# A decoder layer on one core: the convolution table padded from 1408 to 2048 bytes a partition

## The chip, the cores and the metric

One core of a Trainium2 chip runs the kernel in one launch. The metric is the device time of one execution in microseconds (us). In the text, PE is TensorE (matrix products), PEld its loading of stationary operands, DVE is VectorE, ACT ScalarE, POOL GpSimd, SP the queue that issues all the DMAs of this kernel. A matmul has a *stationary* operand (128x128, a slice of the weights) and a *moving* operand (here mostly 128x512 four-byte values, so 2048 bytes of each partition).

## The reference

One layer for 512 positions of width 2048, all in float32:

```python
proj = einsum(rmsnorm(x), w_in)                      # 2048 -> 5376, split into heads of A, B, C
out_a = banded_attention(...)                        # A: 8 heads, window 128, sinks
out_b = stick_breaking_attention(...)                # B: 8 heads
out_c = dilated_attention(...)                       # C: 16 heads, three dilations
mix = concat(rmsnorm(out_a), rmsnorm(out_b), rmsnorm(out_c))
x = x + einsum(mix, w_out)                           # 2048 -> 2048
u = causal_dwconv(einsum(rmsnorm(x), w_up), conv_w, conv_b)   # 2048 -> 2 * 5632, width 3 along the positions
gate, up = split(u, 2)
x = x + einsum(silu(gate) * up, w_down)              # 5632 -> 2048
```

The convolution needs 4 numbers a channel (3 taps and a bias) for 88 tiles of 128 channels: 352 columns of four bytes, 1408 bytes a partition. This is the table of the change.

## The kernel before

Activations lie with channels on the partitions and the 512 positions along the row, so one tile of 128 channels takes 2048 bytes a partition. Every large product is made of three matmuls per tile of 128 input channels, to keep float32 accuracy: the weights and the activations are each split into a high and a low part, and `mm3` (lines 263 to 267) issues high x high, high x low, low x high into one PSUM bank, 512 columns each. `product` (291) makes one output tile out of 16 input tiles (48 matmuls), or of 8 (24 matmuls), or in the last chunk of w_down of 4 (12 matmuls).

The weights come in pieces of 512 KB through the tile `wr` (3 buffers); ACT writes the high half `wh`, DVE the low half `wl` (`split`, 251). The order of all instructions is laid down when the program is built, by a list of tasks with estimated times; it depends on shapes and not on addresses.

The stages, in the order of time:

- The projection w_in with the heads of A, B and C beside it. Moving operands of the projection are the tiles `x` of the pool `xp`.
- The output projection of the heads of B and A (`project_ab`), moving operand again in `x` tiles.
- `fp`, the pool of the rest, is opened at line 908, in the room of the pool `ap` of the attention. Its first tile is the convolution table `conv`. `mix_split` (919) loads the heads of C into tiles `xg2` and splits them into tiles `mc`; the output projection of C then reads `mc` as moving operand, 16 products of 24 matmuls, and `projected` (933) writes the normalised result in `xg2`, high and low.
- The feed-forward: six chunks of up to 8 tiles of 128 channels. A tile of w_up, gate and up side, takes two products of 48 matmuls with moving operand `xg2` (88 products in all). `up` (988) puts silu(gate) * up, high and low, into tiles `x` in chunks 0, 2, 4 and into tiles `mc` in chunks 1, 3, 5 (line 992); the products of w_down (16 per chunk) read them as moving operand. The products of w_down of one chunk run between those of w_up of the next: two of w_up, then two of w_down, and so on.

Where the tiles lie, in bytes from the start of a partition, as the program places them, and the offset modulo 2048 at which they begin:

| tiles | pool | from | modulo 2048 |
|---|---|---|---|
| wr, wh, wl (3 x 4096, 4 x 2048, 4 x 2048) | wp | 10720 | 480 |
| x (32 x 2048) | xp | 39392 | 480 |
| st (9), sq, qs of the attention, 2048 each | ap | 106976 to 139744 | 480 |
| conv (1408) | fp | 104928 | 480 |
| xg2 (32 x 2048) | fp | 106336 | 1888 |
| rg, sq, acc, cv of the feed-forward, 2048 each | fp | 171872 to 225120 | 1888 |
| mc (16 x 2048) | fp | 178016 | 1888 |

A stationary operand is 512 bytes of a partition: slice k of a piece of `wh` or `wl` begins at 480 + 512 k. 480 + 1408 = 1888 is where the offset of the tiles behind `conv` comes from. The pool ends at 227168.

Of the kernel before, what the change touches and what calls it, by code (L numbers as in the profile page):

```python
# [9 lines left out]
F32 = mybir.dt.float32  # L10
# [10 lines left out]
EPS = 1e-6  # L21
NEG = -1e30

# columns of the packed small parameters
SM_AG, SM_FG, SM_MG, SM_G4, SM_SINK, SM_CONV, SM_N = 0, 16, 32, 48, 52, 60, 60 + 88 * 4
# columns of the packed constants
C_ID, C_ONE, C_MASK, C_TRI = 0, 128, 256, 384
NB = 640
# the least spacing of the heads of A, B, C, and what is added to each estimate
GAP = (8, 10, 10)  # L30
MARGIN = 0.08
# the order of the units of A and C
ORDER = "ACACACACCCCC"
# the order in which the output projection takes the tiles of heads: B, A, C
MIX_ORDER = list(range(4, 8)) + list(range(4)) + list(range(8, 16))


class Engine:
    """An engine whose instructions are timed by estimate as they are issued."""

    def __init__(self, clock, engine, cost):
        self.clock, self.engine, self.cost = clock, engine, cost
# [34 lines left out]


class Clock:
    """Issues tasks beside the stream of matrix products, in the order of the estimated times:  # L80
    a task yields when what it has issued has to end before it goes on (or a time to wait)."""

    def __init__(self):
        self.end = 0.0
# [32 lines left out]
def program(tc, xT, w_in, w_out, w_up, w_down, small, table, consts, onehot, lognum, out):  # L117
# [24 lines left out]
    with ExitStack() as ctx:  # L142
# [21 lines left out]
        gacc = [cp.tile([128, S], F32, name="gacc", bufs=2) for _ in range(2)]  # L164
        gacc.append(gacc[1])

        # a slot is taken before its tile is made and given back after the tile's last use
        total = {"pj": 2, "s": 4, "po": 1, "c": 1, "qs": 3, "st": 9, "akv": 4, "vt": 2, "av": 1, "strip": 2,
                 "sc": 3, "pt": 6, "sq": 6, "o": 2, "mx": 3, "dn": 3, "nm": 3, "es": 2,
                 "cv": 3, "acc": 1, "rg": 1}  # L170
        # the shapes of the slots that are not rows
        shapes = {"sc": [128, 1280], "pt": [128, 1664], "vt": [128, 4, 2, 2, 64], "av": [128, 4, 2, 2, 64],
                  "mx": [128, 4], "dn": [128, 4], "nm": [128, 4], "es": [128, 4]}
        free = {tag: list(range(n)) for tag, n in total.items()}
# [27 lines left out]
            slots = [held.pop(id(t)) for t in tiles]  # L202
            spawn(back(slots, max(clock.end - clock.now(), 0.01)))

# [1 line left out]
        b_units = [(10 + p, 6 + p, 14 + p) for p in range(4)]  # L206
        c_units = [(26 + p, 18 + p, 34 + p) for p in range(8)]
        tiles_in = [t for u in b_units[1:] for t in u] + [4, 5]
# [22 lines left out]
        at = {"load": 0, "split": 0, "use": 0}  # L231
# [8 lines left out]
                at["load"] = i + 1  # L240

        def split_next():
            """the next half of a piece of the weights"""
            i = at["split"]
            if i // 2 < len(stream):
                at["split"] = i + 1
                raw, arrival = raws[i // 2]
                n = raw.shape[1] // 2
                spawn(split(raw[:, i % 2 * n:i % 2 * n + n], arrival, i))
# [22 lines left out]
            return grab(ps, "pj")  # L272

        def accumulate(pt, acts, ks, each=None):
            """the k tiles ks of a tile of a product, with the next weights of the stream"""
            half = min(len(acts), 8) // 2
            for k in ks:
                while acts[k] not in ready:
                    idle()
                if k % half == 0:  # L280
                    while at["use"] not in parts:
                        idle()
                    hi, lo = parts.pop(at["use"])
                    at["use"] += 1
                    split_next()
                mm3(pt, hi, lo, k % half, ready[acts[k]], k == 0, k == len(acts) - 1)
                if each:
                    each(k)
                clock.run()

        def product(acts, after):
            """one tile of a product; then the task after(tile)"""
            pt = begin()
            accumulate(pt, acts, range(len(acts)))
            spawn(after(pt))
            clock.run()

# [1 line left out]
        def rstd(pool, ss, n):  # L299
            """-2n * (ss / n + EPS) ** -0.5, with a Newton step after the tables"""  # L300
            y, a = yield from take(pool, "sq", 2)
            scalar.activation(y, ss, AF.Ln, bias=epsc, scale=1.0 / n)
            scalar.activation(y, y, AF.Exp, scale=-0.5)
            yield
            gpsimd.tensor_mul(a, y, y)
            yield
            vector.scalar_tensor_tensor(a, ss, n * EPS, a, op0=ALU.add, op1=ALU.mult)
            give(ss)
            vector.scalar_tensor_tensor(a, a, -3.0 * n, y, op0=ALU.add, op1=ALU.mult)
            give(y)  # L310
            return a
# [28 lines left out]
        vector.memset(epsc, EPS)  # L340
        vector.memset(onec, 1.0)

# [1 line left out]
        with ExitStack() as actx:  # L344
            ap = actx.enter_context(tc.tile_pool(name="ap", bufs=1))

            def strips():
                """the biases of the heads that softmax takes, in their order, as far ahead as there is room"""
                for head in strip_order:
                    g = yield from take(ap, "strip")  # L350
                    a = rb[head:head + 1, 0:1]
                    load(g, bass.AP(tensor=a.tensor, offset=a.offset, ap=[[1, 128], [1, S]]))
                    yield
                    ready["strip", head] = g
# [6 lines left out]
            HALF = (slice(0, 64), slice(64, 128))  # L361

            def stacked(q, key):
                """for each head of the pair its high parts over its low parts"""
                res = yield from take(ap, "st", 2, F32R)
                for h in range(2):
                    scalar.copy(res[h][HALF[h]], q[HALF[h]])
                yield
                for h in range(2):
                    vector.tensor_sub(res[h][HALF[1 - h]], q[HALF[h]], res[h][HALF[h]].bitcast(F32))  # L370
                give(q)
                yield
                ready[key] = res

            def doubled(q, key):
                """for each head of the pair its high parts twice and its low parts twice"""
                tag = "akv" if key[0] == "ak" else "st"
                res = yield from take(ap, tag, 4, F32R)
                res = [res[:2], res[2:]]
                for h in range(2):  # L380
                    scalar.copy(res[h][0][HALF[h]], q[HALF[h]])
                yield
                for h in range(2):
                    vector.tensor_sub(res[h][1][HALF[h]], q[HALF[h]], res[h][0][HALF[h]].bitcast(F32))
                give(q)
                yield
                for x in range(2):
                    for h in range(2):
                        load(res[h][x][HALF[1 - h]].bitcast(F32), res[h][x][HALF[h]].bitcast(F32))
                    yield  # L390
                yield
                ready[key] = res
# [72 lines left out]
            def softmax_head(q, dup, vt, h, o, head, sinks, window):  # L465
# [52 lines left out]

                def place(t, i, n):
                    if window:  # L520
                        # block (j, i) at 256 j + 128 (i - j), the last one after its zeros
                        base, step = ((0, 128), (128, 128), (384, 128), (640, 256))[i]
                    else:
                        # block (j, i) at 384 j + 128 i
                        base, step = 128 * i, 384
                    b = t[:, base:base + 1]
                    return bass.AP(tensor=b.tensor, offset=b.offset, ap=[b.ap[0], [step, n // 128], [1, 128]])
# [29 lines left out]
                yield  # L557
                yield from head_out(po, h, o)

            # key blocks j of the stick-breaking heads: (j, first query, number of queries, column); in the operands of  # L560
            # products the last block follows columns of zeros
            BLK = [(0, 0, 512, 0), (1, 128, 384, 512), (2, 256, 256, 896), (3, 384, 128, 1152)]
            WIDE = [(0, 512, 0), (128, 384, 512), (256, 256, 896), (256, 256, 1408)]

# [78 lines left out]
                yield  # L643
                yield from head_out(po, h, o)

            # heads in the order in which they run, at most three at a time
            heads = []
            running = {"n": 0, "last": -100}
            outs = {}
# [40 lines left out]
                return stick_head(q[h], k[h], vt, h, o)  # L690

            def spill(g):
                """the normalised heads of a group in high and low parts, to wait for the slots of x"""
                tiles = (range(4), range(4, 8))[g]
                rg = yield from take(ap, "acc")
                yield from row_rstd(ap, gacc[g], 128 * len(tiles), rg)
# [26 lines left out]
                    strip_order.append(head)  # L723
            spawn(starter())

            # x and the first three tiles of w_in, tile of x by tile of x
            acc = grab(ap, "o")
            xg = [("x", k) for k in range(KT)]
            first = [grab(ps, "s"), grab(ps, "s"), grab(ps, "s")]
# [112 lines left out]
            spilled = []  # L842

            def last_products(q_after, v_after):
                """the last two tiles, by halves of x, so that half of its slots are free early"""
                q, v = begin(), begin()
                accumulate(q, xg, range(8))
                accumulate(v, xg, range(8), mix_load)
# [25 lines left out]
                else:  # L874
                    product(xg, normed(0, False, stacked, ("aq", p)))

            # the output projection of the heads of B and A, beside the last heads of C
            xn = []

            def project_ab(m):  # L880
# [20 lines left out]
            while left[2]:  # L901
# [2 lines left out]
                    m += 1  # L904
                else:
                    idle()
# [1 line left out]
        fp = ctx.enter_context(tc.tile_pool(name="fp", bufs=1, reuse_waits="tile"))  # L908
        cv = fp.tile([128, SM_N - SM_CONV], F32, name="conv")
        load(cv, small[:, SM_CONV:])  # L910

        rg = []

# [42 lines left out]
        for m in range(KT):  # L956
            product([("mix", i) for i in MIX_ORDER[8:]], projected(m))

# [1 line left out]
        gs = {}  # L960

        def conv(t, f, use):
# [80 lines left out]


def _pieces(w):
    """[K, N] as pieces of eight K tiles by one N tile, each [128, 8 * 128]"""
    k, n = w.shape
    w = w.reshape(k // 1024, 8, 128, n // 128, 128).transpose(3, 0, 2, 1, 4)
    return np.ascontiguousarray(w).reshape(n // 128 * (k // 1024), 128, 1024)
# [48 lines left out]
```

## Time and profile before

| | us |
|---|---|
| median of 3 runs (2267.1 to 2267.99) | 2267.95 |
| span of the profiled execution, first to last instruction | 2265.6 |
| PE busy in it | 2254.7 |
| DVE busy | 1211.2 |
| ACT busy | 981.9 |
| output projection of C (`mc` moving) | 700.38 to 789.97 |
| feed-forward | 789.97 to the end |

The busy time of PE counts a matmul from its start to its modelled end, and matmuls overlap, so that a stretch of back-to-back matmuls shows 100% whatever its pace. The pace is read from starts: the time from the start of one matmul to the start of a later one, divided by the number of matmuls begun between them.

### The profile page before, as it was taken

To read this page: it belongs to the slowest core of one execution; us is meant where nothing else is said; L and a number is where in the kernel's file an instruction comes from. 1 tells how busy PE (TensorE), PEld (TensorE's weight loads), DVE (VectorE), ACT (ScalarE), POOL (GpSimd) and SP (SyncE) were. 2 spreads that over 40 slices of the span, in tenths; PEclk is the share of its full clock that TensorE was granted. 3 is DMA by queue.
4 is the path that set the end of the run, shared out by engine and by line. 5 is a ranking of instruction groups with operands and counts; after the bars stand their busy time and mean duration, and the time that the engine had idled before them with its cause. 6 is when DMAs were issued, how large, how long until landed. Compare 5 with 4: busy or idle time off the path is not lost.

```text
span 2265.6 us, 27033 instructions
## 1 busy us (share of the span) xinstructions
PE 2254.7 (100%) x10068; PEld 1838.4 (81%) x10068; DVE 1211.2 (53%) x2090; ACT 981.9 (43%) x1864; POOL 100.8 (4%) x153
## 2 busy tenths in 40 slices
PE   8999999999999999999999999999999999999999
PEld 6888888888888878888888888888888888888887
DVE  7667777767755654544444444444444444443444
ACT  6778677776654433333323323332333233232322
POOL 4000101010100200000000000000000000000000
PEclk9999999999999999999999999999999999999999
DMA  6333343334743333323333322333332233333224
GB/s 196 95 94 98 121 146 112 110 103 162 227 159 98 93 94 94 98 96 93 93 95 100 94 93 93 93 93 94 101 94 93 93 93 96 97 95 94 93 86 137
DMA packets 83082, 244.26 MB, mean 108 GB/s; under 512 B 9784, under 2 KB 13240, under 8 KB 82952
## 3 DMA queue, kind: packets, MB, share of 16 engines
q1 hardware_dynamic: 82952, 242.55, 34.3%
q8 instruction: 79, 1.29, 0.2%
q14 instruction: 51, 0.42, 0.1%
HBM read 223.05 MB, written 12.64 MB: 104 GB/s over the span
## 4 chain that ended last, share of the span: by engine, by line
PE 98%; DMA 0%; DVE 0%; issue 0%; SPq 0%; ACT 0%; DVEq 0%; ACTq 0%
PE pj L49 92%; PE s L49 4%; PE po L49 2%; PE c L49 1%; SPq L127 0%; DMA st<-in_xT_dram 0%; DVE wl L49 0%; DMA wr<-in_w_in_dram 0%; DMA cst<-in_consts_dram 0%; ACT x L49 0%; DVE sq L49 0%; DVE x L49 0%; DVE o L49 0%; DVE pt L49 0%; DVE sc L49 0%
## 5 line engine op out<-in xcount | busy, mean ns | idle before, releaser
L49 ACT CAST wh<-wr 128x512 fp32r<-128x512 f32 (+2 forms) x782 | 475.3, 609 | 1114.8 <-PE pj L49 1031.9
L49 PE MATMUL pj<-xg,wh 128*128 128x512 f32 x2816 | 885.1, 395 | 0.0
L49 DVE TENSOR_TENSOR wl<-wr,wh 128x512 fp32r<-128x512 f32 (+2 forms) x782 | 539.4, 692 | 536.0 <-ACT wh L49 530.2
L49 PE MATMUL pj<-x,wh 128*128 128x512 f32 x2272 | 710.2, 394 | 0.0
L49 PEld LDWEIGHTS pj<-xg,wh 128*128 128x128 f32 x2816 | 528.6, 188 | 128.6 <-issue 0.5
L49 PE MATMUL pj<-xg,wl 128*128 128x512 f32 x1408 | 556.2, 395 | 0.0
L49 PEld LDWEIGHTS pj<-x,wh 128*128 128x128 f32 x2272 | 415.3, 188 | 81.4 <-issue 3.0
L49 PE MATMUL pj<-x,wl 128*128 128x512 f32 x1136 | 444.1, 391 | 0.0
L49 PEld LDWEIGHTS pj<-xg,wl 128*128 128x128 f32 x1408 | 264.3, 188 | 64.1
L49 PE MATMUL pj<-mc,wh 128*128 128x512 f32 x896 | 281.5, 395 | 0.0
L49 PEld LDWEIGHTS pj<-x,wl 128*128 128x128 f32 x1136 | 213.2, 188 | 46.1
L49 PEld LDWEIGHTS pj<-mc,wh 128*128 128x128 f32 x896 | 168.2, 188 | 40.9
L49 PE MATMUL pj<-mc,wl 128*128 128x512 f32 x448 | 177.0, 395 | 0.0
L49 DVE TENSOR_TENSOR x<-pj,x 128x512 f32<-128x512 f32 x112 | 77.4, 691 | 133.8 <-PE pj L49 133.8
L49 DVE SCALAR_TENSOR_TENSOR cv<-sq,conv,cv 128x511 f32<-128x511 f32 (+1 forms) x176 | 132.1, 751 | 28.2 <-ACT cv L49 25.1
L49 DVE TENSOR_TENSOR sq<-pj,r 128x512 f32<-128x512 f32 x88 | 60.9, 692 | 146.5 <-PE pj L49 146.4
L49 PEld LDWEIGHTS pj<-mc,wl 128*128 128x128 f32 x448 | 84.1, 188 | 20.5
L49 ACT ACTIVATE cv<-sq,conv 128x512 f32<-128x512 f32 x88 | 71.9, 817 | 29.0 <-DVE sq L49 29.0
L49 DVE CUSTOM_DVE_ANT_0 sc<-s,strip 128x128 f32<-128x128 f32 (+3 forms) x96 | 43.6, 455 | 75.5 <-PE s L49 75.2
L49 ACT ACTIVATE sc<-sc,nm 128x128 f32<-128x128 f32 (+2 forms) x96 | 50.2, 526 | 1.4 <-DVE nm L49 1.3
L49 ACT CAST pt<-s 128x128 fp32r<-128x128 f32 (+2 forms) x96 | 35.7, 398 | 26.8 <-PE s L49 26.3
L49 ACT ACTIVATE sc<-sc,dn 128x128 f32<-128x128 f32 (+2 forms) x96 | 43.5, 526 | 4.3 <-DVE dn L49 4.2
(115 smaller groups left out, 1316.6 us busy)
## 6 DMA issues: line engine op xcount, KB each, us to landing
wr<-in_w_up_dram SPq DMA_DIRECT2D x176, 512.0 KB, 3.5
wr<-in_w_down_dram SPq DMA_DIRECT2D x80, 512.0 KB, 3.4
wr<-in_w_in_dram SPq DMA_DIRECT2D x78, 512.0 KB, 3.6
wr<-in_w_out_dram SPq DMA_DIRECT2D x32, 512.0 KB, 3.5
st<-st SPq DMA_DIRECT2D x48, 128.0 KB, 4.4
strip<-rb SPq DMA_DIRECT2D x24, 256.0 KB, 4.0
st<-in_xT_dram SPq DMA_DIRECT2D x16, 256.0 KB, 3.9
o_dram<-o SPq DMA_DIRECT2D x16, 256.0 KB, 4.3
```

Source lines behind the costliest of these rows:

```text
L49: res = issue(out, *args, **kwargs)
```

## The change

`conv` is made 512 columns wide instead of 352; the load fills its first 352 columns as before, and the reads (`cv[:, 4 * t + i]`) stay in those. The 640 bytes more a partition are never written or read. The tiles of `fp` behind `conv` move up by 640 bytes: they begin at 1888 + 640 = 2528, that is 480 modulo 2048; the pool ends at 227808 instead of 227168. The diff drops comments besides, which the program does not contain.

```diff
         fp = ctx.enter_context(tc.tile_pool(name="fp", bufs=1, reuse_waits="tile"))
-        cv = fp.tile([128, SM_N - SM_CONV], F32, name="conv")
-        load(cv, small[:, SM_CONV:])
+        cv = fp.tile([128, 512], F32, name="conv")
+        load(cv[:, :SM_N - SM_CONV], small[:, SM_CONV:])
```

## Rows read from the trace of the kernel before

**Rows 1.** The page: span, busy time by engine, granted clock in 40 slices.
```profile
span 2265.6 us, 27033 instructions
...
PE 2254.7 (100%) x10068; PEld 1838.4 (81%) x10068; DVE 1211.2 (53%) x2090; ACT 981.9 (43%) x1864; POOL 100.8 (4%) x153
...
PEclk9999999999999999999999999999999999999999
...
PE 98%; DMA 0%; DVE 0%; issue 0%; SPq 0%; ACT 0%; DVEq 0%; ACTq 0%
```
**Rows 2.** Timeline of PE: start, length, instruction; ends of runs of one moving tile.
```profile
992.43 0.63 PE L49 MATMUL pj<-x,wh 128*128 128x512 f32 x2
...
1003.33 0.62 PE L49 MATMUL pj<-xg,wh 128*128 128x512 f32 x2
...
1025.72 0.63 PE L49 MATMUL pj<-x,wh 128*128 128x512 f32 x2
...
1258.73 0.63 PE L49 MATMUL pj<-mc,wh 128*128 128x512 f32 x2
...
1269.93 0.63 PE L49 MATMUL pj<-xg,wh 128*128 128x512 f32 x2
```
**Rows 3.** Windows: PE, PEld, DVE, ACT, POOL busy (count), clock, DMA share, GB/s.
```profile
992.43:1258.73 266.30, 266.30 (x1154) 216.24 (x1152) 119.28 (x176) 81.68 (x129) 0.00 (x0) 1.00 0.31 95
1258.73:1527.53 268.80, 268.80 (x1154) 216.22 (x1152) 119.22 (x176) 81.76 (x129) 0.00 (x0) 1.00 0.31 94
```
**Rows 4.** Windows of two stretches whose products have x as moving operand throughout.
```profile
120.59:129.44 8.85, 8.85 (x40) 7.32 (x39) 6.13 (x13) 8.56 (x20) 0.00 (x0) 1.00 0.45 109
674.54:700.38 25.84, 25.84 (x116) 21.40 (x114) 15.47 (x24) 11.42 (x20) 1.04 (x1) 1.00 0.50 166
```
**Rows 5.** Groups of PE by line, tiles and shape: count, busy time and mean.
```profile
L49 PE MATMUL pj<-xg,wh 128*128 128x512 f32 x2816 | 885.1, 395 | 0.0
...
L49 PE MATMUL pj<-xg,wl 128*128 128x512 f32 x1408 | 556.2, 395 | 0.0
L49 PE MATMUL pj<-x,wl 128*128 128x512 f32 x1136 | 444.1, 391 | 0.0
L49 PE MATMUL pj<-mc,wh 128*128 128x512 f32 x896 | 281.5, 395 | 0.0
L49 PE MATMUL pj<-mc,wl 128*128 128x512 f32 x448 | 177.0, 395 | 0.0
```
**Rows 6.** Timeline of PE: two heads of B, both operands in tiles st.
```profile
120.13 0.62 PE L49 MATMUL s<-st,st 128*128 128x512 f32 x2
120.59 0.62 PE L49 MATMUL pj<-x,wh 128*128 128x512 f32 x2
...
644.87 0.62 PE L49 MATMUL s<-st,st 128*128 128x512 f32 x2
645.32 0.39 PE L49 MATMUL pj<-x,wh 128*128 128x512 f32 x1
```
**Rows 7.** Timeline of PE: the first matmuls after those of a head of C.
```profile
662.07 0.63 PE L49 MATMUL pj<-x,wh 128*128 128x512 f32 x2
...
663.46 0.61 PE L49 MATMUL pj<-x,wh 128*128 128x512 f32 x2
```
**Rows 8.** Timelines of SP, of DVE and of PE where fp is opened.
```profile
668.76 0.42 SPq L127 DMA_DIRECT2D conv<-in_small_dram  x1
...
669.75 5.15 SPq L127 DMA_DIRECT2D xg<-o_dram  x8
...
685.40 1.41 DVE L49 SCALAR_TENSOR_TENSOR mc<-xg,sm,mc 128x512 fp32r<-128x512 f32 x2
...
700.38 0.62 PE L49 MATMUL pj<-mc,wh 128*128 128x512 f32 x2
```
**Rows 9.** What SP waited for from 800 to 2260 us: total, times, longest.
```profile
SPq L127 <- DVE wl L49: 1348.8, 269, 7.6
```

## The prediction

> **What bounds the kernel now.** The page comes first: PE is busy for the whole span, makes up 98% of the chain that ended last, and has the full clock (2.4 GHz) granted in every slice; DVE is busy for half of it and ACT for less [rows 1]. So the time is the sum of the spaces between the starts of matmuls, and only what changes a space, or puts a hole between two, moves the end. The mean length of a matmul in the groups can't tell spaces, as ends are modelled: 395 ns for the products on `xg2` and `mc`, 391 for those on `x` [rows 5].
>
> The second view is therefore PE's timeline, read at the places where the moving tile changes [rows 2]. In the feed-forward, two products on `x` (48 matmuls) take 1003.33 - 992.43 = 10.90 us, 227.1 ns a matmul. The next two on `xg2` (96) take 22.39 us, 233.2 ns. Later two on `mc` (48) take 11.20 us, 233.3 ns. Same code, same engines beside it, same weights' buffers: only the moving tile differs. Longer stretches say it more exactly [rows 3]: eight rounds of 96 matmuls on `xg2` and 48 on `mc` (1152 weight loads, one for each matmul) take 268.80 us, 233.33 ns each; eight rounds with `x` in place of `mc` take 266.30, with the same DVE, ACT and DMA work to within 0.1 us. The 2.50 us between them are 384 matmuls that are 6.5 ns cheaper. A stretch on `x` alone, the last of the projection of B and A, has 114 matmuls in 25.84 us: 226.7 ns [rows 4].
>
> What sets `x` apart from `xg2` and `mc`? By the table of addresses, `x` begins at 480 modulo 2048, as the weights do, and the other two at 1888. Nothing else that I can see goes with the pace: `mc` and `x` take turns at the same job.
>
> **The change, part by part.**
>
> The load of `conv` moves the same 1408 bytes a partition in one DMA, before the eight loads of the heads of C [rows 8]; ACT and DVE read the same 352 columns. Cost nothing: no instruction is added, removed or reordered, as the order does not depend on addresses.
>
> The tiles of `fp` move by 640 bytes over the dead tiles of the attention, so a tile may have to wait for another old tile than before. The last old tile is free when the last head of C has been stored, ahead of `conv`'s load at 668.76. What follows has cover: the last `mc` tile of the projection of C is written by 685.40 + 1.41 = 686.81, and PE first needs `mc` at 700.38 [rows 8]; until then it works on `x`. A new wait up to 13.6 us long would cost nothing; were that cover gone, each us would cost one. I take 0.
>
> The matmuls whose moving operand moves from 1888 to 480 modulo 2048: 2816 + 1408 on `xg2` and 896 + 448 on `mc`, 5568 in all [rows 5]. Before, each takes 233.33 ns [rows 3]. What they take after is not in the trace, since no `fp` tile lies at 480; the nearest rows bound it. From above, nothing would change, 233.33. Within the feed-forward, `x` at 480 in runs of 48 takes 227.1 [rows 2]; unbroken, 226.7 [rows 4]. After a break the pace is not there at once: six matmuls on `x` behind a head's last take 663.46 - 662.07 = 1.39 us, 232 ns each [rows 7]. After the change every product behind 700 us has its moving operand at 480, and no switch is left to break the run, so I take the unbroken 226.7. Gain: 5568 x 6.63 ns = 36.9 us; with 227.1, 34.7 us. The x products of the feed-forward might win their 0.4 ns too, 1152 x 0.4 = 0.5 us, left out. A gain below 226.7 is excluded by nothing but is shown by no row.
>
> Does the high address matter rather than the offset? `x` lies below 104928 and `xg2`, `mc` above. The tiles `st` of the attention lie at 106976 to 125408, where `xg2` lies, but at 480 modulo 2048. Two matmuls on them take 0.46 us at 120.13 and 0.45 us at 644.87 [rows 6], so 225 to 230 ns each (starts are given to 10 ns). That is nearer to `x` than to `xg2`, and I take the offset as the cause. 230 stays as a bound: 5568 x 3.33 = 18.5 us.
>
> DVE, ACT and the weights must follow the faster pace. A piece of 512 KB is used by 24 matmuls, 5.60 us before and 5.44 after. The stretch on `x` alone runs at that pace with nothing late [rows 4], and SP, which reloads the weights, waits for DVE to free a buffer in 269 loads, not the other way about [rows 9]. Nothing is late next: PE stays the bound at its new pace. The last product, its addition and the store are as before.
>
> Sum against the profiled execution: 2265.6 - 36.9 = 2228.7 us of span. The median lies 2.35 us above the span, which I keep: 2231.0 us.
>
> A rule of the Trainium skill speaks against this change. "SBUF — State Buffer", section "Who interferes with whom", says that "PE and ACT never wait on anyone", and the specifications of that page give 16-byte lines as the only grain of an address; 480 and 1888 are both multiples of 16, so by that page the move is worth 0 and the time stays. The rows do not sit well with it: something makes one moving tile 6.5 ns dearer than another in the same job, and the page names nothing that could.
>
> **The rivals.**
>
> *Not the offset.* The 6.5 ns belong to something else in which `x` differs from `fp`'s tiles (the place in the memory, or the pool's other tiles), and it moves along. Then 2268.0, no change; this is also the result of the page's rule above. For it: no `fp` tile was ever at 480. Against it: the `st` rows [rows 6], and that `xg2` and `mc`, tens of KB apart, have one pace [rows 2].
>
> *Half of it.* The offset counts, but in the upper part the pace only falls to the 230 ns of the dearer `st` pair: 2267.95 - 18.5 = 2249.4.
>
> *Slower: sharing an offset with the tiles of ACT and DVE is what costs.* In the feed-forward `sq`, `cv`, `acc` lie at 1888 with `xg2` and `mc`, and ACT and DVE stream through them while PE reads; `x` would be cheap because it is alone at 480 with `wr`, `wh`, `wl`. After the change all of them are at 480: `xg2` and `mc` keep 233.3, and the x products of the feed-forward (1152) rise from 227.0 to 233.3: 7.3 us, 2275.2. It turns into a loss as soon as the second half outweighs the first, and passes 0.2% (4.5 us) when those products rise by 3.9 ns. Against it: in the attention `sq` and `qs` lie at 480 with `x`, and from 120.59 to 129.44, where ACT is busy for 8.56 of 8.85 us, 39 matmuls take 226.9 ns each [rows 4].
>
> **How the numbers follow.** The offset at its full price 0.84 (2228.5 to 2236), half of it 0.06 (2249), not the offset 0.06 (2268), slower 0.04 (2275). The time is that of the first: 2231.0. The range reaches from a little below the sum to 2240, which takes in 227.1 ns (2233.3), a run that falls back to 232 ns for six matmuls after each of the 152 products that move (152 x 6 x 5.3 ns = 4.8 us, 2235.8) and the 0.1% by which runs differ; the rest, 0.16, is left out. A measurement of this kernel can tell about 0.2% from no change. Faster by more than that (below 2263.4) holds the first two, 0.90; the same 0.06; slower 0.04.
>
> **What would show it right or wrong.** In the profile after, PE's timeline should show 96 matmuls on `xg` in 21.77 us instead of 22.39, 48 on `mc` in 10.88 instead of 11.20, and the rounds with `mc` and with `x` should take the same 261.2 us. The projection of C should shrink from 89.59 us to 87.1. Up to 700 us nothing should move. If `xg` and `mc` stay at 233 and `x` too, the cause is elsewhere; if `x` rises to 233, it is the sharing with ACT and DVE. A hole on PE between 700 and 710 us would mean a wait at the opening of `fp` that I did not see. The prediction fails if the pace depends on which tiles follow one another rather than on where each begins.

## The result and the profile after

The changed kernel takes 2230.61 us (median of 4 runs, 2230.36 to 2231.09) against 2267.86 for the kernel before beside it: a ratio of 0.9837, 95% interval 0.9823 to 0.9851, 37.25 us less. The forecast was 2231.0. The profiled execution spans 2229.3 us.

The profile's page of the changed kernel shows the same instructions, the full clock and DVE and ACT as busy as before ([rows 1]); only PE's busy time has shrunk, by 36.9 us:

```profile
span 2229.3 us, 27033 instructions
...
PE 2217.8 (99%) x10068; PEld 1839.1 (82%) x10068; DVE 1211.4 (54%) x2090; ACT 983.4 (44%) x1864; POOL 100.7 (5%) x153
...
PEclk9999999999999999999999999999999999999999
```

The timeline of PE where the moving tile changes, which answers to [rows 2]:

```profile
985.08 0.61 PE L49 MATMUL pj<-x,wh 128*128 128x512 f32 x2
...
995.96 0.61 PE L49 MATMUL pj<-xg,wh 128*128 128x512 f32 x2
...
1017.72 0.62 PE L49 MATMUL pj<-x,wh 128*128 128x512 f32 x2
...
1246.20 0.62 PE L49 MATMUL pj<-mc,wh 128*128 128x512 f32 x2
...
1257.08 0.62 PE L49 MATMUL pj<-xg,wh 128*128 128x512 f32 x2
```

48 matmuls on `x` take 10.88 us, 96 on `xg2` 21.76 (22.39 before), 48 on `mc` 10.88 (11.20 before). The three tiles have one pace, 226.7 ns. The windows of the eight rounds with `x` and the eight with `mc`, which answer to [rows 3], and of the projection of the heads of C (columns as there: length, then PE, PEld, DVE, ACT, POOL busy and count):

```profile
985.08:1246.20 261.12, 261.12 (x1154) 216.33 (x1152) 119.31 (x176) 81.95 (x129) 0.00 (x0) 1.00 0.31 97
1246.20:1507.32 261.12, 261.12 (x1154) 216.35 (x1152) 119.30 (x176) 82.06 (x129) 0.00 (x0) 1.00 0.31 97
701.32:788.36 87.04, 87.04 (x386) 72.11 (x384) 53.42 (x78) 38.72 (x62) 18.09 (x14) 1.00 0.32 97
```

Both rounds take 261.12 us for 1152 matmuls, 226.67 ns each, where they took 266.30 and 268.80. The projection of C lasts 87.04 us instead of 89.59 (700.38 to 789.97). Where `fp` is opened, nothing has come up: the timelines of SP, DVE and PE, which answer to [rows 8], are shifted by the 0.94 us by which this execution reached the place later, and no more. All runs below but one (`e5_x_fp_moved`) reach the first matmul on `mc` between 700.5 and 701.3 us, so a shift of this size is the spread between runs.

```profile
669.70 0.42 SPq L127 DMA_DIRECT2D conv<-in_small_dram  x1
...
670.69 5.13 SPq L127 DMA_DIRECT2D xg<-o_dram  x8
...
686.33 1.41 DVE L49 SCALAR_TENSOR_TENSOR mc<-xg,sm,mc 128x512 fp32r<-128x512 f32 x2
...
701.32 0.62 PE L49 MATMUL pj<-mc,wh 128*128 128x512 f32 x2
```

### The profile page after: what moved, and what is told of

Its sections match the earlier page's. It is cut to its first block, busy times and chain, and to the rows that moved or that the text cites. A ratio compares the mean times of both kernels' runs of the same rounds, so it can differ in the third digit from the quotient of the medians.

```text
span 2229.3 us, 27033 instructions
## 1 busy us (share of the span) xinstructions
PE 2217.8 (99%) x10068; PEld 1839.1 (82%) x10068; DVE 1211.4 (54%) x2090; ACT 983.4 (44%) x1864; POOL 100.7 (5%) x153
## 4 chain that ended last, share of the span: by engine, by line
PE 99%; SPq 0%; DVE 0%; DMA 0%; issue 0%; ACT 0%; ACTq 0%; DVEq 0%
PE pj L49 91%; PE s L49 5%; PE po L49 2%; PE c L49 1%; SPq L127 0%; DVE wl L49 0%; DMA st<-in_xT_dram 0%; DMA cst<-in_consts_dram 0%; DVE sq L49 0%; DVE x L49 0%; DVE o L49 0%; DVE pt L49 0%; ACT x L49 0%; DVE sc L49 0%; ACT wh L49 0%
## 5 line engine op out<-in xcount | busy, mean ns | idle before, releaser
L49 PE MATMUL pj<-xg,wh 128*128 128x512 f32 x2816 | 867.9, 390 | 0.0
L49 PE MATMUL pj<-xg,wl 128*128 128x512 f32 x1408 | 548.3, 389 | 0.0
L49 PE MATMUL pj<-mc,wh 128*128 128x512 f32 x896 | 276.1, 389 | 0.0
```

The lines of the kernel that those rows point to most:

```text
L49: res = issue(out, *args, **kwargs)
```

## The experiments

The time was as forecast, but the forecast left open what "480 modulo 2048" means. Theory R: what counts is the *distance* between where the moving tile and the weights begin. Theory A: what counts is the moving tile's own offset of 480. Open for both: whether the period is 2048 or less. Each diff is against the changed kernel. An unused tile is given one `memset` of one column, which is all the work it adds. The runs were single executions, but for the last; the kernel before ran beside them and took 2267.67 to 2268.33 us.

**Other distances that are multiples of 256.** `e1_plus512`:

```diff
-        cv = fp.tile([128, 512], F32, name="conv")
+        cv = fp.tile([128, 640], F32, name="conv")
```

> The table is made 2560 bytes wide, so xg2 and mc begin at 992 modulo 2048, 512 behind the weights. Theory R (the distance between the moving tile and the weights counts) with a period of 512: xg2 and mc keep 226.7 ns a matmul, about 2231 us. R with the period 2048 that the change names: they fall back towards 233.3 ns, up to 2268 us. Theory A (the moving tile's own offset of 480 counts, wherever the weights lie): 2231 with a period of 512, up to 2268 with one of 2048. x stays at 226.7 ns in all of them.

Measured: 2230.93 us. `e2_plus256`, with 576 columns:

> The table is made 2304 bytes wide, so xg2 and mc begin at 736 modulo 2048, 256 behind the weights. If the period is 256 bytes or less, 226.7 ns a matmul and about 2231 us; if it is 512 or more, by R and A alike, they are out of step: about 233.3 ns, 2268 us.

Measured: 2230.29 us. The window of the eight rounds with `mc`, for `e1_plus512` and then for `e2_plus256`:

```profile
1246.03:1507.15 261.12, 261.12 (x1153) 216.22 (x1152) 119.33 (x176) 82.02 (x129) 0.00 (x0) 1.00 0.31 97
```
```profile
1245.39:1506.51 261.12, 261.12 (x1154) 216.22 (x1152) 119.34 (x176) 82.03 (x129) 0.00 (x0) 1.00 0.31 97
```

Both are as fast as the changed kernel to 0.01 us over 1152 matmuls, with `xg2` and `mc` at 992 and at 736. So the period is not 2048: 256 and 512 are both in step. Nor can it be 128 or a divisor of that, since the 1408 of the kernel before is 11 x 128 and was dear.

**The weights moved, and everything moved.** `e3_weights_x_moved` moves the weights and `x` by 640 and takes the table back to 1408 bytes:

```diff
         gacc.append(gacc[1])
+        pad = cp.tile([128, 160], F32, name="pad")
+        nc.vector.memset(pad[:, :1], 0.0)
...
-        cv = fp.tile([128, 512], F32, name="conv")
+        cv = fp.tile([128, 352], F32, name="conv")
```

> The table stays at 1408 bytes and 640 unused bytes lie ahead of the weights: wr, wh, wl and x begin at 1120, xg2 and mc at 480. R: x is in step with the weights (226.7 ns), xg2 and mc lie 1408 behind them as in the kernel before (233.3 ns), 2268 us. A: xg2 and mc at 480 are cheap (226.7), x at 1120 is dear, 3552 matmuls by 6.6 ns or 23 us, so 2254 us.

Measured: 2267.58 us. `e4_all_moved` has the same pad and keeps the table at 512 columns:

> As the changed kernel (table of 2048 bytes), with 640 unused bytes ahead of the weights: weights, x, xg2 and mc all begin at 1120. R: all in step, 226.7 ns, 2231 us. A: nothing lies at 480, 233.3 ns for the 5568 matmuls on xg2 and mc and the 3552 on x: 2231 + 37 + 23 = 2291 us.

Measured: 2230.57 us. The windows of the rounds with `x` and with `mc` of `e3_weights_x_moved`, then that with `mc` of `e4_all_moved`:

```profile
992.61:1258.92 266.31, 266.31 (x1154) 216.25 (x1153) 119.30 (x176) 81.64 (x129) 0.00 (x0) 1.00 0.31 95
1258.92:1527.72 268.80, 268.80 (x1154) 216.22 (x1153) 119.22 (x176) 81.77 (x129) 0.00 (x0) 1.00 0.30 94
```
```profile
1245.67:1506.79 261.12, 261.12 (x1153) 216.22 (x1152) 119.30 (x176) 82.14 (x129) 0.00 (x0) 1.00 0.32 97
```

In the first, `xg2` and `mc` lie at 480, as in the changed kernel, and are as dear as in the kernel before, whose rounds took 266.30 and 268.80 [rows 3]. In the second nothing lies at 480, and all is cheap. Theory A has fallen; the distance decides. (In both runs the small tiles ahead of the weights stay where they were, and `x` keeps its pace all the same, so those are not what it has to be in step with.)

**The partner.** In all these runs `x` kept its distance to the weights. `e5_x_fp_moved` parts them, with a pad between:

```diff
         wp = ctx.enter_context(tc.tile_pool(name="wp", bufs=2))
+        qp = ctx.enter_context(tc.tile_pool(name="qp", bufs=1))
         xp = ctx.enter_context(tc.tile_pool(name="xp", bufs=1))
...
         gacc.append(gacc[1])
+        pad = qp.tile([128, 160], F32, name="pad")
+        nc.vector.memset(pad[:, :1], 0.0)
```

> The changed kernel with 640 unused bytes between the weights and x: wr, wh, wl stay at 480, x, xg2, mc and the tiles of the attention begin at 1120, 640 (128 modulo 256) behind the weights. Theory R, the weights are the partner: all 9120 matmuls of the large products are out of step; 5568 on xg2 and mc by 6.66 ns are 37 us, 1152 on x in the feed-forward 7.7 us, 2400 on x before 700 us up to 16 us: 2283 to 2291 us. Rival, the partner of xg2 and mc is x (or another tile that moves with them): 2231 us.

Measured: 2281.84 us, 13.7 more than the kernel before. The windows of the rounds with `x` and with `mc`, and the first matmul of the projection of C:

```profile
999.35:1268.15 268.80, 268.80 (x1153) 216.22 (x1152) 119.21 (x176) 81.63 (x129) 0.00 (x0) 1.00 0.31 94
1268.15:1536.95 268.80, 268.80 (x1153) 216.22 (x1152) 119.22 (x176) 81.72 (x129) 0.00 (x0) 1.00 0.30 94
...
707.69 0.64 PE L49 MATMUL pj<-mc,wh 128*128 128x512 f32 x2
```

`xg2` and `mc` are in step with `x` and dear all the same, and now `x` is dear too: both rounds take 268.80 us. So the partner lies among `wr`, `wh`, `wl`. It also answers the prediction's last doubt, whether the pace depends on which tiles follow one another: here every moving tile of the large products begins at the same offset, and all are dear.

The total came out below the 2283 to 2291 expected. The stretch before the projection of C was the term too large: it grew from 700.38 to 707.69, 7.3 us, where 2400 matmuls had been put down at up to 16. There the runs on `x` are broken by the matmuls of the heads, and behind a break the pace is dear at any distance [rows 7]. Counted from the starts of all matmuls on `x` before 700 us (spaces over 300 ns left out), the first three behind a break take 232.0 ns in the kernel before and 232.0 in `e5_x_fp_moved`, the next three 229.4 and 232.6, the next six 227.9 and 232.1, later ones 227.2 and 233.0. The wrong distance thus costs a matmul its full price only far from a break. The spaces behind the 2400 matmuls add up to 6.65 of the 7.3 us.

Who uses the weights' buffers besides PE? The DMA writes `wr`, ACT reads it and writes `wh`, DVE writes `wl`. In the kernel before there is a stretch on `xg2` in which all three rest, but for the last 0.03 us of ACT:

```profile
1346.93:1348.33 1.40, 1.40 (x8) 1.13 (x6) 0.00 (x0) 0.03 (x1) 0.00 (x0) 1.00 0.00 0
```

Six matmuls (a weight load each, x6) take 1.40 us, 233.3 ns each, the full price. That leaves PE's own reads of `wh` and `wl` as the partner, by elimination.

**The tiles of ACT and DVE.** `e6_xg2_0_mc_96` moves `mc`, `sq`, `cv` and `acc` by 96 bytes and leaves `xg2` in step:

```diff
             rg.append((yield from take(fp, "rg")))
+            pad = fp.tile([128, 24], F32, name="pad")
+            nc.vector.memset(pad[:, :1], 0.0)
```

> The changed kernel with 96 unused bytes between xg2 and mc: xg2 at distance 0 from the weights, mc and the tiles sq, cv, acc that ACT and DVE use at distance 96. R, only the moving tile of a matmul and the weights count: xg2 at 226.7 ns, mc at its own price between 226.7 and 233.3, 2231 to 2239.5 us. Rival, the distance of the tiles of ACT and DVE counts: xg2 dearer than 226.7 too, up to 2268 us.

Measured: 2240.96 us, 1.5 above the upper end. The windows of the rounds with `x` and with `mc`:

```profile
987.69:1248.81 261.12, 261.12 (x1154) 216.22 (x1152) 119.24 (x176) 82.06 (x129) 0.00 (x0) 1.00 0.31 97
1248.81:1512.91 264.10, 264.10 (x1153) 216.26 (x1152) 119.18 (x176) 82.05 (x129) 0.00 (x0) 1.00 0.31 96
```

With `x` and `xg2` in step the rounds keep 261.12 us, though ACT and DVE now work on tiles 96 bytes off: where those lie costs PE nothing. The rounds with `mc` lose 2.98 us over 384 matmuls, 7.8 ns each. That is more than the price of the distance, as three further windows of this run show: the projection of C, 384 matmuls on `mc` without a switch, then one run of 48 on `mc` in a round and the 96 on `xg2` behind it.

```profile
701.31:790.93 89.62, 89.62 (x386) 72.09 (x384) 53.41 (x78) 38.70 (x62) 18.16 (x14) 1.00 0.31 94
1248.81:1260.02 11.21, 11.21 (x49) 9.02 (x48) 6.66 (x10) 3.79 (x6) 0.00 (x0) 1.00 0.31 95
1260.02:1281.82 21.80, 21.80 (x97) 18.02 (x96) 8.24 (x12) 6.46 (x11) 0.00 (x0) 1.00 0.33 97
```

Unbroken, a matmul at distance 96 takes 233.4 ns, as at 128. The rest are the switches: the 48 on `mc` take 11.21 us instead of 11.20, and the 96 on `xg2`, in step themselves, 21.80 instead of 21.76, some 0.05 us a switch from `xg2` to `mc` and back. The feed-forward has 16 of those, 0.8 to 0.9 us, which the expectation of 2239.5 had not counted; what is left of the 1.5 is within the 0.7 us by which runs of one kernel differ.

**The other distances.** `e7_plus32`, `e8_plus64`, `e9_plus128` and `e10_plus192` make the table 520, 528, 544 and 560 columns wide.

> The table is 2080 bytes wide: xg2 and mc begin 32 bytes behind the weights modulo 256, the weights and x as in the kernel before. Theory R, all or nothing (only multiples of 256 are in step): 233.3 ns a matmul on xg2 and mc, 2268 us. Theory R, graded (the price grows with the distance up to 128): between 226.7 and 233.3, a quarter of the way, 228.3 ns, 2240 us.

Measured: 2268.61 us.

> The table is 2112 bytes wide: distance 64 modulo 256. All or nothing: 233.3 ns, 2268 us. Graded: half way, 230 ns, 2249 us. If the period is 64, 226.7 ns and 2231 us; but then the 1408 bytes of the kernel before, 22 times 64, would have been in step, which they were not.

Measured: 2244.47 us.

> The table is 2176 bytes wide: distance 128 modulo 256, as 1408 is (5 times 256 and 128), at another place in the memory. R with a period of 256: as in the kernel before, 233.3 ns, 2268 us. If the distance modulo 2048 were what counts, and only 1408 were bad: anything, 2231 us among it.

Measured: 2267.94 us.

> The table is 2240 bytes wide: distance 192 modulo 256, 64 from the other side. All or nothing: 233.3 ns, 2268 us. Graded and symmetric: as distance 64, 230 ns, 2249 us; graded by the distance forward: three quarters, 231.7 ns, 2259 us or beyond.

Measured: 2268.32 us. `e11_xg2_224_mc_160` makes the table 568 columns wide and puts a pad of 48 columns at the place of that of `e6_xg2_0_mc_96`:

> xg2 at distance 224 and mc at 160 modulo 256 from the weights, which fills in the distances not yet seen. From 32 and 192 (233.3 ns) against 64 (229.0): if 64 is the exception, both at 233.3 and 2268 us; if multiples of 32 alternate, or nearness to 256 helps, less: from 2231. A pace below 226.7 would beat the changed kernel.

Measured: 2269.65 us. The window of the rounds with `mc` of each, in the order 32, 64, 128, 192, and of `e11_xg2_224_mc_160`:

```profile
1259.56:1528.35 268.79, 268.79 (x1153) 215.89 (x1152) 119.17 (x176) 81.70 (x129) 0.00 (x0) 1.00 0.30 94
```
```profile
1250.87:1514.55 263.68, 263.68 (x1153) 216.35 (x1152) 119.26 (x176) 82.15 (x129) 0.00 (x0) 1.00 0.30 96
```
```profile
1259.27:1528.07 268.80, 268.80 (x1153) 216.25 (x1152) 119.25 (x176) 82.02 (x129) 0.00 (x0) 1.00 0.30 94
```
```profile
1259.49:1528.29 268.80, 268.80 (x1153) 215.42 (x1152) 119.23 (x176) 81.85 (x129) 0.00 (x0) 1.00 0.30 94
```
```profile
1259.93:1529.05 269.12, 269.12 (x1153) 216.63 (x1152) 119.26 (x176) 81.79 (x129) 0.00 (x0) 1.00 0.30 94
```

In `e11_xg2_224_mc_160` the two distances are told apart by the projection of C (384 matmuls on `mc`, at 160) and by the first 96 on `xg2`, at 224, of the rounds above:

```profile
701.06:791.02 89.96, 89.96 (x385) 72.33 (x384) 53.42 (x78) 38.73 (x62) 18.08 (x14) 1.00 0.30 94
1271.17:1293.57 22.40, 22.40 (x97) 18.04 (x96) 8.24 (x12) 6.43 (x11) 0.00 (x0) 1.00 0.32 94
```

Each window divided by its matmuls (1152 for the rounds), with the distance modulo 256:

| distance | ns a matmul | from |
|---|---|---|
| 0 | 226.67 | the changed kernel, `e1_plus512`, `e2_plus256`, `e4_all_moved`, `e12_1536` below |
| 32 | 233.3 | `e7_plus32` |
| 64 | 228.9 | `e8_plus64` |
| 96 | 233.4 (`mc`, projection of C) | `e6_xg2_0_mc_96` |
| 128 | 233.33 | the kernel before, `e3_weights_x_moved`, `e5_x_fp_moved`, `e9_plus128` |
| 160 | 234.3 (`mc`, projection of C) | `e11_xg2_224_mc_160` |
| 192 | 233.3 | `e10_plus192` |
| 224 | 233.3 (`xg2`) | `e11_xg2_224_mc_160` |

Of the two rules in the expectations, "all or nothing" holds for 32, 96, 128, 160, 192 and 224 and fails at 64, which gives back two thirds of the price; "graded" fails at 32, and 64 has no counterpart at 192. The distance of 32 at its full price was the plainest miss of the graded rule: 2240 expected, 2268.6 measured. Why 64 is an exception stays open. No distance beat 226.67 ns.

**The smallest table that is in step.** `e12_1536` adds 128 bytes instead of 640:

```diff
-        cv = fp.tile([128, 512], F32, name="conv")
+        cv = fp.tile([128, 384], F32, name="conv")
```

> The table is 1536 bytes wide, 128 bytes more than in the kernel before instead of 640: xg2 and mc at 2016, 1536 = 6 times 256 behind the weights. R with a period of 256: 226.7 ns, 2231 us, as the changed kernel. If 2048, 512 or 256 as a forward distance had only been enough by chance, more, up to 2268.

Measured: 2230.70 us (median of 4, 2230.60 to 2231.11), ratio 0.9836 with a 95% interval of 0.9819 to 0.9852. It is as fast as the changed kernel in a fifth of the room. No version was faster than these two by more than the 0.7 us by which runs of one kernel differ.

## Why the prediction was right

*The bound and the way to read it* were right: the time is the sum of the spaces between starts on PE, and these fell where the moving tile was moved and, but for some 0.3 us on `x`, nowhere else in the chain.

*The main term*, 5568 matmuls by 6.63 ns: measured 233.33 to 226.67, 6.66 ns, which is 37.1 us. By stages, the projection of C gave 2.55 us. From the first matmul of the feed-forward (789.97 before, 788.36 after) to the end of the span, 1475.6 us became 1440.9, which is 34.7 less. The stretch before the projection came out 0.94 us longer in this execution, so that the spans differ by 36.3. Taking the unbroken pace rather than the 227.1 ns of the short runs was the right choice: with no switch left, the `x` products of the feed-forward fell to 226.7 as well. The 0.5 us left out for them came to some 0.3: by the starts, the 1152 matmuls on `x` in the feed-forward took 226.93 ns on average before and 226.67 after.

*The terms at nothing* held: the table's load, the moved tiles' waits and the weights' supply show nothing new on PE.

*The rivals.* That it is not the offset: gone with the result, 2230.6 against 2268. With it goes what had been drawn from the Trainium skill ("SBUF — State Buffer", section "Who interferes with whom"), that the move would be worth 0. The sentence quoted from there, "PE and ACT never wait on anyone", is not refuted by these runs: PE paid the full price in the stretch where ACT, DVE and the DMA rested. What failed is the step from it to a price of 0: PE did go faster or slower by an address, which that page of the Trainium skill does not count. Half of it: `xg2` and `mc` reach 226.67 in the upper part too, so the 230 ns of the dearer `st` pair was not the pace of that memory; it fits the pace behind a break, where those two matmuls stand. Slower by sharing an offset with ACT's and DVE's tiles: `x` stayed at 226.7 with all of them at 480, and `e6_xg2_0_mc_96` parts the two with no loss for `xg2`.

*What the prediction had too narrow* is the cause. It spoke of the offset of 480 modulo 2048. The runs show a distance to the weights' buffers, and a period of 256: the kernel before was slow because 1408 is 5 x 256 + 128, and any table of a multiple of 256 bytes would have done. The sum did not hang on it, since a padding to 2048 met both readings; that the cause was only half known and the number right all the same was luck of that choice.

*What stays open.* That the partner is the stationary operand as PE reads it follows by elimination, from one stretch of six matmuls; `wr`, `wh` and `wl` moved together in every run, so `wh` and `wl` were not told apart. Why a distance costs some 6.7 ns, why 64 costs a third of it, and whether distances that are not multiples of 32 do anything else, no run shows.

## What to carry to other kernels

Where PE is the bound and 100% busy, read its pace from the starts of matmuls, one group of moving tiles against another; a busy share does not show a difference of 3%, and the mean lengths showed a part of it (395 against 391 ns [rows 5] for 233.3 against 227). If two tiles of the same shape in the same job have two paces, compare the addresses at which they begin with that of the weights, modulo 256, and pad a small tile ahead of them until the distance is a multiple of 256. This was seen with matmuls of 128x512 four-byte values, each with its own weight load; other shapes and types were not tried. An odd-sized table at the head of a pool moves everything behind it.

## What had not been expected of the hardware

That the pace of a stream of matmuls depends on the distance between the moving tile and the weights' buffers modulo 256 bytes: 226.67 ns at 0, 228.9 at 64, 233.3 to 234.3 at the other multiples of 32. And that a break in the stream costs beyond itself: before 700 us the first three matmuls behind one took 232 ns on average and the next three 229.4 before the pace came near 227, in the stretch of [rows 7] all six 232, so that the same wrong distance cost 7.3 us in the stretch with the attention, where full price was expected to be up to 16.
